# Half of retention's gate columns as four more block-product pairs, and most later modulation columns made in attention

## The chip, the cores and the metric

The kernel runs on one core of a Trainium2 chip. The metric is the device time of one execution in microseconds; 2243.01 us is the median of three runs of the kernel before (2242.38 to 2244.39). Five engines of the core run their own instruction queues and wait for each other by semaphores: TensorE (PE) multiplies, VectorE (DVE) and ScalarE (ACT) do elementwise work, GpSimd (POOL) does some elementwise work and issues some DMAs, SyncE (SP) issues nearly all other DMAs. Each engine takes its instructions in the order in which the program wrote them.

## The reference, cut to what matters

One decoder block in float32 over 1024 tokens of width 1024. The parts that the change touches:

```python
mod = jax.nn.silu(c) @ w_ada + b_ada                    # 6 x 1024 modulation columns
sh1, sc1, g1, sh2, sc2, g2 = jnp.split(mod, 6, axis=-1)
h = modulate(rms_norm(x, norm1_g), sh1, sc1)
parts = jnp.split(h @ w_in, IN_OFFSETS, axis=-1)
rq, rk, rv, rg = parts[0], parts[1], parts[2], parts[3] # rg: 4 heads x 512 gate columns
ro = retention(rotary(rq), rotary(rk) / 16, rv)         # 4 heads, chunks of 128 tokens, a running state
ro = group_norm(ro) * gn_g + gn_b
ret_out = (jax.nn.silu(rg) * ro) @ w_ret_out
att_out = dilated attention of 3 groups x 4 heads       # from parts[4:13]
merged = sigmoid(gate_a) * ret_out + sigmoid(gate_b) * att_out
x = x + g1 * (merged @ w_o)
x = x + g2 * (relu(modulate(rms_norm(x), sh2, sc2) @ w1) ** 2 @ w2)
```

Of `mod`, only sh1 and sc1 are needed at the start; the other four (32 tiles of 128 columns, `later_mods`) are first read after attention.

## The kernel before

**Precision.** Every float32 product is made of three matmuls on rounded operands: each operand is split into a high part (`hi`, rounded by a ScalarE copy) and a low part (`lo = x - hi`, a VectorE subtraction), and `mm3` (L197 to L205) adds lo*hi, hi*lo and hi*hi in PSUM. A weight tile of 128x1024 is split so by `split_w` (L188): one ScalarE copy (L191), one VectorE subtraction (L192).

**Stages in order of time.** Attention values (`av_step`); block products (`queries_keys`, running `PAIRS` through the `Blocks` class `BA`); retention values (`values`); retention itself, 4 heads of 8 chunks (`chunk`); attention, two pairs of heads (`att_step`, `cover_step`, `gate_step`); output projections; MLP.

**Block products.** A pair is 256 columns of `h @ w`. Instead of eight half-size products `Blocks` makes seven (`ORDER`, with sums of the operands), each of four groups of three matmuls 128x128x512, so 84 matmuls for a pair; the plain way (`proj_mm`) takes 96 for the same columns. `PAIRS` has 18 pairs: 8 of retention's queries and keys (`r`), 6 of attention's queries (`a`), 4 of the branch gates (`g`). `a_out` (L902) writes a pair's result; gates get a sigmoid and go to DRAM.

**Retention, one chunk** (`chunk`, L673). TensorE runs in this order: the state's products of this chunk `kv` (6 matmuls), a part of the gate projection `rg` (`proj_mm`), the scores `sT` and transposed keys `kT` of the next chunk (`s_kt`), the output `o` (9 matmuls), the transposes `oT` of the chunk before, another part of `rg`. VectorE runs in this order: the state's update (L699), the loads prepared ahead (a split of a gate weight tile, a modulation column), `sm`, `sml`, `kl` of the next chunk's scores and keys, `statel` (L713), the group norm's statistics and its result `onm` (L723 to L729), and in four chunks of each later head the product with the gate (L670). PSUM tiles of kind `s` are a ring of four, six are taken per chunk; `sT` of the next chunk takes the bank of the `o` that `onm` of the chunk before has read. Each head has four gate weight tiles (128 columns each, two chunks for a tile, 24 matmuls per chunk), and each chunk one modulation column (`mod_prep`, L450: one VectorE pass of 128x1024 and two small instructions).

**Loads.** `Steps` (L48) issues all weight, query and modulation loads in one flat order through a ring `raw` of three buffers of 128x1024 (512 KB); a load is issued when the one three places earlier has been used. Before a step's body, `prepare` uses the loads of the next step, and then the next step's successor's loads as long as these are weights. What it writes for ScalarE and VectorE (splits, `q_prep`, `mod_prep`) stands ahead of the body's own instructions.

**Attention.** `combos` gives six steps to each pair of heads. Step i makes the keys of combination i (`proj_gen`, 48 matmuls, then `k_split`: `kh` on ScalarE, `kl` on VectorE L1213) and, woven between them, the scores of combination i-1 (`scores_gen`), whose biases VectorE adds (L1243); `scores_end` takes maxima (VectorE) and exponentials (ScalarE, L1266). A step i > 0 loads a weight tile and the queries of combination i-1 (`q_prep`: `qh` L1203, `ql` L1204). After combinations 1 and 3 `stats_out` writes the statistics to DRAM and reads them back on SP's queue (L1324, L1325): the second waits there until the first has landed. During the first pair of heads `result_sums` runs sums of retention's results between DRAM tensors on POOL's DMA queue.

Of the kernel before, what the change touches and what calls it, by code (L numbers as in the profile page):

```python
# [11 lines left out]
F32 = mybir.dt.float32  # L12
# [5 lines left out]
P = 128  # L18
# [116 lines left out]
def block_kernel(ctx, tc, io, stop=None, dbg=None):  # L135
# [36 lines left out]
    dsh = cst.tile([P, NK // 2], F32, name="dsh")  # L172

# [141 lines left out]
    cb = right0.tile([P, 1024], F32, name="cb")  # L315
# [206 lines left out]
    def etile(name, dt=F32):  # L522
        return R["p"].tile([P, 1024], dt, tag="E", bufs=12, name=name)
# [149 lines left out]
    def chunk(h, c, ahead, w=None):  # L673
# [19 lines left out]
        if g > 0:  # L693
            proj_mm(hd["rgp"], hd["rgw"], ks[:2])
# [23 lines left out]
        if g > 0:  # L718
            proj_mm(hd["rgp"], hd["rgw"], ks[2:])
# [161 lines left out]
    PAIRS = [{"r": r_pairs, "a": a_pairs, "g": g_pairs}[i].pop(0) for i in "rargrargrargrargaa"]  # L881
# [3 lines left out]
    def a_load(q, part):  # L885
        pair = PAIRS[q]
        src = io[{"g": "w_gate2", "a": "w_aq"}.get(pair[0]) or f"w_r{pair[1]}"]
# [19 lines left out]
    def a_out(q, n, x, y=None):  # L907
# [12 lines left out]
        f = AF.Sigmoid if pair[0] == "g" else AF.Copy  # L920
        if y is None:
            nc.scalar.activation(o, view(x), f)
        else:
            (nc.vector.tensor_add if n == "12" else nc.vector.tensor_sub)(o, view(x), view(y))
            if pair[0] == "g":
                nc.scalar.activation(o, o, f)
        if n in ("12", "21"):
            if pair[0] == "g":
                dst = gate_d[GATES[2 * pair[1] + i]]
            elif pair[0] == "a":  # L930
                dst = aq_d[pair[2], pair[1], i]
            else:
                return
            nc.sync.dma_start(dst, OA[q][i])
# [15 lines left out]

    gate_d = [dram.tile([P, S], F32, name=f"gated{i}") for i in range(16)]
# [375 lines left out]
    def weights(pair):  # L1327
# [5 lines left out]
        pr = p.tile([P, 3, 8, 2], F32, tag="pr", name=f"pr{pair}")  # L1333
        sm = p.tile([P, 8, 2], F32, tag="ssum", name=f"ssum{pair}")
# [6 lines left out]
        for g in range(3):  # L1341
            nc.vector.tensor_mul(pr[:, g], wt[:, g], stn[g][:, :, 2:4])
        nc.vector.tensor_add(sm, pr[:, 0], pr[:, 1])
        nc.vector.tensor_add(sm, sm, pr[:, 2])
# [1058 lines left out]
def pack(x, c, w_ada, b_ada, norm1_g, w_in, rel_bias, ret_gn_g, ret_gn_b,  # L2403
# [3 lines left out]
    att = w[:, 6144:10752].reshape(1024, 3, 3, 512)  # L2407
    gates = lambda js: np.concatenate([w[:, 10752 + P * j:10752 + P * j + P] for j in js], axis=1)
# [12 lines left out]
        "w_rg": _cols(w[:, 4096:6144]),  # L2421
# [31 lines left out]
```

## Time and profile before

| what | value |
|---|---|
| median of three runs | 2243.01 us |
| the profiled execution, span | 2248.9 us |
| granted TensorE clock, mean | 0.993 |
| block products, first to last matmul | 159.5 to 503.8 us |
| retention, first `kv` to the first matmul of attention | 676.1 to 982.5 us |
| key steps of the first pair of heads, to the first gate matmul behind them | 982.5 to 1070.4 us |
| key steps of the second pair, to the first gate matmul behind them | 1142.3 to 1230.9 us |

The profile is of one execution, 2248.9 us from its first to its last instruction, 5.9 us (0.26%) over the median of the timed runs. A row of the instruction view gives start, duration, engine, line, operation, output and inputs, and in brackets how long the engine stood idle before it and who ended that. A row of the waits view gives who waited for whom: total us, times, longest. A row of the windows view gives the busy time of PE, PE's weight loads, DVE, ACT and POOL in a stretch, the granted clock and the DMA share. Durations of neighbours on one engine overlap a little, so costs are best read from start to start.

### The profile page before, as it was taken

How to read it: one execution, taken by the hardware profiler on the slowest of the kernel's cores; microseconds unless marked ns; L12 is line 12 of the kernel's file. 1: busy time of each engine (PE TensorE's matmuls, PEld its weight loads, DVE VectorE, ACT ScalarE, POOL GpSimd, SP SyncE). 2: the span in 40 equal slices, each digit the busy share in tenths (PEclk: the TensorE clock that was granted, in tenths of full speed). 3: DMA queues.
4: the chain of work that ended last, by engine and by line, in shares of the span. 5: the costliest groups of instructions: out<-in, count | busy, mean ns of one | idle time of the engine just before them, and what ended most of it. 6: DMA issues, size and time to landing. Idle time of an engine off the chain costs nothing.

```text
span 2248.9 us, 27131 instructions
## 1 busy us (share of the span) xinstructions
PE 2183.6 (97%) x10130; PEld 1808.0 (80%) x10130; DVE 1455.3 (65%) x2285; ACT 908.6 (40%) x1665; POOL 145.6 (6%) x168
## 2 busy tenths in 40 slices
PE   7999999999999999999999999999999999999998
PEld 5887888887877888887788788888778888888887
DVE  6527777753548778853554554576866665787845
ACT  4323333223334445534634633434454445533412
POOL 0001111000011122100000000002100000000003
PEclk9999999999999999999999999999999999999999
DMA  9648999625775556549723345645134443745322
GB/s 361 197 145 277 289 284 287 198 93 178 246 271 169 168 181 206 191 165 241 207 78 94 105 178 210 247 156 178 61 136 155 155 155 145 266 151 169 122 85 76
DMA packets 154371, 408.93 MB, mean 182 GB/s; under 512 B 27062, under 2 KB 54973, under 8 KB 149822
## 3 DMA queue, kind: packets, MB, share of 16 engines
q1 hardware_dynamic: 148542, 363.14, 46.3%
q0 software_dynamic: 5696, 44.04, 8.2%
q8 instruction: 80, 1.31, 0.2%
q14 instruction: 53, 0.43, 0.1%
HBM read 316.27 MB, written 156.13 MB: 210 GB/s over the span
## 4 chain that ended last, share of the span: by engine, by line
PE 47%; DVE 5%; ACT 2%; DMA 2%; issue 1%; SPq 0%; POOL 0%; POOLq 0%; DVEq 0%; ACTq 0%
PE fp L201 4%; PE fp L203 4%; PE fp L205 4%; PE f2a L203 2%; PE f2a L205 2%; PE f2a L201 2%; PE ak L201 1%; PE ak L203 1%; PE ak L205 1%; PE wo L201 1%; PE wo L205 1%; PE wo L203 1%; PE roa L203 1%; PE roa L201 1%; PE roa L205 1%
## 5 line engine op out<-in xcount | busy, mean ns | idle before, releaser
L201 PE MATMUL qap<-hh,qaw 128*128 128x512 f32 x216 | 84.3, 390 | 3.9 <-ACT qat L280 2.2
L205 PE MATMUL qap<-hh,qaw 128*128 128x512 f32 x216 | 84.1, 389 | 0.0
L203 PE MATMUL qap<-hl,qaw 128*128 128x512 f32 x216 | 84.0, 389 | 0.0
L614 POOL TENSOR_TENSOR j<-qk,j 128x512 fp32r<-128x512 f32 x32 | 43.4, 1356 | 470.2 <-ACT j L613 470.2
L1912 ACT ACTIVATE a<-a 128x512 f32<-128x512 f32 x48 | 30.3, 631 | 79.1 <-DVE a L1911 79.1
L1266 ACT ACTIVATE P<-P,ng 128x128 f32<-128x128 f32 (+1 forms) x96 | 41.9, 438 | 41.8 <-DVE ng L1263 41.8
L1809 POOL TENSOR_TENSOR accnf<-accnf,sqnf 128x256 f32<-128x256 f32 (+1 forms) x18 | 16.6, 922 | 619.0 <-ACT sqnf L1808 619.0
L258 DVE TENSOR_TENSOR fw<-w1r,fw 128x512 fp32r<-128x512 f32 x48 | 33.0, 688 | 36.3 <-ACT fw L248 36.3
L2098 ACT CAST w2h<-w2s 128x512 fp32r<-128x512 f32 x36 | 22.4, 621 | 77.6 <-DVE w2s L2136 75.3
L201 PEld LDWEIGHTS qap<-hh,qaw 128*128 128x128 f32 x216 | 40.5, 188 | 13.2 <-ACT qat L280 2.6
L201 PE MATMUL fp<-h2h,fw 128*128 128x512 f32 x128 | 50.0, 390 | 0.0
L203 PE MATMUL fp<-h2l,fw 128*128 128x512 f32 x128 | 49.8, 389 | 0.0
L205 PE MATMUL fp<-h2h,fw 128*128 128x512 f32 x128 | 49.8, 389 | 0.0
L201 PE MATMUL roa<-rh,rwl 128*128 128x512 f32 x128 | 49.8, 389 | 0.0
L203 PE MATMUL roa<-rl,rwh 128*128 128x512 f32 x128 | 49.8, 389 | 0.0
L205 PE MATMUL roa<-rh,rwh 128*128 128x512 f32 x128 | 49.8, 389 | 0.0
L636 ACT COPY sm<-sT 128x128 f32<-128x128 f32 x32 | 8.5, 267 | 101.8 <-PE sT L627 100.1
L1647 DVE TENSOR_TENSOR rwl<-rwl,rwh 128x1024 fp32r<-128x1024 f32 x25 | 30.2, 1221 | 29.0 <-ACT rwh L1677 29.0
L1809 POOL TENSOR_TENSOR accn<-accn,sqn 128x512 f32<-128x512 f32 x12 | 15.5, 1296 | 491.8 <-ACT sqn L1808 491.8
L205 PEld LDWEIGHTS qap<-hh,qaw 128*128 128x128 f32 x216 | 40.5, 188 | 8.4
L203 PEld LDWEIGHTS qap<-hl,qaw 128*128 128x128 f32 x216 | 40.5, 188 | 8.3
L1204 DVE SCALAR_TENSOR_TENSOR ql<-raw,qh 128x1024 fp32r<-128x1024 f32 x12 | 14.7, 1224 | 47.6 <-ACT qh L1203 47.6
(3081 smaller groups left out, 7216.7 us busy)
## 6 DMA issues: line engine op xcount, KB each, us to landing
v<-vd SPq DMA_DIRECT2D x32, 512.0 KB, 5.4
raw<-in_w_ada_dram SPq DMA_DIRECT2D x32, 512.0 KB, 4.9
w1r<-in_w_ff_dram SPq DMA_DIRECT2D x32, 512.0 KB, 5.1
vd<-vo SPq DMA_DIRECT2D x24, 512.0 KB, 6.4
yt<-y POOLq DMA_DIRECT2D x6, 2048.0 KB, 15.0
xsd<-as SPq DMA_DIRECT2D x24, 512.0 KB, 2.7
w2r<-in_w_ff2s_dram SPq DMA_DIRECT2D x24, 512.0 KB, 7.1
em<-in_w_ada_dram SPq DMA_DIRECT2D x16, 512.0 KB, 10.2
```

Of the source, the lines that this page charges most:

```text
L201: nc.tensor.matmul(o, wl, xh, start=first, stop=False, skip_group_check=skip)
L203: nc.tensor.matmul(o, wh, xl, start=False, stop=False, skip_group_check=skip)
L205: nc.tensor.matmul(o, wh, xh, start=False, stop=last, skip_group_check=skip)
L258: nc.vector.tensor_sub(t[:, 512:], src, fv(t[:, :512]))
L614: nc.gpsimd.tensor_sub(t[:, 1], src, fv(t[:, 0]))
L636: nc.scalar.copy(sm, ps[:, :C])
L1204: nc.vector.scalar_tensor_tensor(lo, raw, QSCALE, fv(hi), op0=ALU.mult, op1=ALU.subtract)
L1266: nc.scalar.activation(v, v, AF.Exp, bias=ng[:, blk:blk + 1], accum_out=st[:, g, blk, 2 + a:3 + a])
L1647: nc.vector.tensor_sub(lo, fv(lo), fv(hi))
L1809: (nc.vector if f == 7 else nc.gpsimd).tensor_add(G["acc", key], G["acc", key], sq)
L1912: nc.scalar.activation(o, o, AF.Relu)
L2098: nc.scalar.copy(hi, src)
```

## The change

Each head's 512 gate columns are cut in two. The first 256 stay in retention as two weight tiles instead of four; a tile now serves four chunks, with 12 matmuls per chunk instead of 24. The other 256 become one pair for each head in the block products, kind `s`, with a Silu at the end; the results go to DRAM (`srg_d`) and are read back in chunks 4 and 5 of the head. `PAIRS` has 22 entries instead of 18, in another order. Modulation columns are loaded with chunks 2, 5 and 7 of a head (12 in all) and two each with steps 1 to 5 of both attention pairs (20). The tile `cb` (Silu of c) lives on into attention, and two small tiles of `weights` are folded into others to make room.

```diff
+    cb = cst.tile([P, 1024], F32, name="cb")
...
-    cb = right0.tile([P, 1024], F32, name="cb")
...
-        if c % 2 == 0:
+        if c % 4 == 0:
             hd["rgw"] = w
             hd["rgp"] = ps_mm(f"rg{h}{c}")
-        ks = range(4 * (c % 2), 4 * (c % 2) + 4)
+        if c in (4, 5):
+            hd["srg", h, c - 2] = etile(f"srg{h}{c - 2}")
+            nc.sync.dma_start(hd["srg", h, c - 2], srg_d[h][c - 4])
+        ks = range(2 * (c % 4), 2 * (c % 4) + 2)
...
-            proj_mm(hd["rgp"], hd["rgw"], ks[:2])
+            proj_mm(hd["rgp"], hd["rgw"], ks[:1])
...
-            proj_mm(hd["rgp"], hd["rgw"], ks[2:])
+            proj_mm(hd["rgp"], hd["rgw"], ks[1:])
...
-        if c % 2 == 1:
-            hd["srg", h, c // 2] = etile(f"srg{h}{c // 2}")
-            nc.scalar.activation(hd["srg", h, c // 2], flat(hd["rgp"]), AF.Silu)
+        if c % 4 == 3:
+            hd["srg", h, c // 4] = etile(f"srg{h}{c // 4}")
+            nc.scalar.activation(hd["srg", h, c // 4], flat(hd["rgp"]), AF.Silu)
...
-    PAIRS = [{"r": r_pairs, "a": a_pairs, "g": g_pairs}[i].pop(0) for i in "rargrargrargrargaa"]
+    s_pairs = [("s", h) for h in range(H)]
+    PAIRS = [{"r": r_pairs, "a": a_pairs, "g": g_pairs, "s": s_pairs}[i].pop(0) for i in "rsrarsrarsrarsraggagga"]
...
-        f = AF.Sigmoid if pair[0] == "g" else AF.Copy
+        f = {"g": AF.Sigmoid, "s": AF.Silu}.get(pair[0], AF.Copy)
...
-            if pair[0] == "g":
+            if pair[0] in "gs":
                 nc.scalar.activation(o, o, f)
...
+            elif pair[0] == "s":
+                dst = srg_d[pair[1]][i]
...
+    srg_d = [[dram.tile([P, S], F32, name=f"srgd{h}{i}") for i in range(2)] for h in range(H)]
...
-                      ([wsplit(io["w_rg"][4 * h + c // 2])] if c % 2 == 0 else []) + [mod_load(later_mods[8 * h + c])],
-                      manual=True)
+                      ([wsplit(io["w_rg"][2 * h + c // 4])] if c % 4 == 0 else []) +
+                      ([mod_load(later_mods.pop(0))] if c in (2, 5, 7) else []), manual=True)
...
-                      ([(aq_d[pair, *combos[i - 1]], q_prep(pair, *combos[i - 1]))] if i > 0 else []),
+                      ([(aq_d[pair, *combos[i - 1]], q_prep(pair, *combos[i - 1]))] if i > 0 else []) +
+                      [mod_load(later_mods.pop(0)) for _ in range(2 if i > 0 else 0)],
                       manual=i == pair == 0)
```

More of the change, by code (lines that the diff above doesn't have):

```diff
@@ L886, in a_load @@
         pair = PAIRS[q]
-        src = io[{"g": "w_gate2", "a": "w_aq"}.get(pair[0]) or f"w_r{pair[1]}"]
+        src = io[{"g": "w_gate2", "a": "w_aq", "s": "w_rg2"}.get(pair[0]) or f"w_r{pair[1]}"]
         i = 2 * pair[1] + pair[2] if pair[0] == "a" else pair[-1]
@@ L1332, in weights @@
         wt = p.tile([P, 3, 8, 2], F32, tag="wt", name=f"wt{pair}")
-        pr = p.tile([P, 3, 8, 2], F32, tag="pr", name=f"pr{pair}")
-        sm = p.tile([P, 8, 2], F32, tag="ssum", name=f"ssum{pair}")
         wg = p.tile([P, 2, 8, 2], F32, tag="wg", name=f"wg{pair}")
@@ L1341, in weights @@
         for g in range(3):
-            nc.vector.tensor_mul(pr[:, g], wt[:, g], stn[g][:, :, 2:4])
-        nc.vector.tensor_add(sm, pr[:, 0], pr[:, 1])
-        nc.vector.tensor_add(sm, sm, pr[:, 2])
+            nc.vector.tensor_mul(stn[g][:, :, 2:4], wt[:, g], stn[g][:, :, 2:4])
+        sm = mx
+        nc.vector.tensor_add(sm, stn[0][:, :, 2:4], stn[1][:, :, 2:4])
+        nc.vector.tensor_add(sm, sm, stn[2][:, :, 2:4])
         nc.vector.reciprocal(sm, sm)
@@ L2420, in pack @@
         "w_rv": _vblocks(w[:, 2048:4096]),
-        "w_rg": _cols(w[:, 4096:6144]),
+        "w_rg": _cols(rg[:, :, :256].reshape(1024, 1024)),
+        "w_rg2": _pairs(rg[:, :, 256:].reshape(1024, 1024)),
         "w_aq": _pairs(att[:, :, 0].reshape(1024, 1536)),
```

1 line of the change is left out of this document (added).

## The prediction

> **What bounds the kernel now.** First the page's busy times, then the windows of the stages that the change touches.
>
> ```profile
> span 2248.9 us, 27131 instructions
> ...
> PE 2183.6 (97%) x10130; PEld 1808.0 (80%) x10130; DVE 1455.3 (65%) x2285; ACT 908.6 (40%) x1665; POOL 145.6 (6%) x168
> ```
>
> ```profile
> 160.00:503.00 343.00, 339.08 (x1495) 280.12 (x1494) 246.33 (x386) 103.54 (x178) 33.88 (x48) 1.00 0.78 243
> 753.00:830.00 77.00, 77.00 (x378) 64.00 (x377) 62.42 (x132) 37.27 (x93) 15.17 (x16) 1.00 0.58 192
> 985.00:1070.00 85.00, 78.17 (x402) 65.87 (x400) 36.96 (x41) 37.74 (x94) 5.78 (x7) 0.99 0.89 256
> 1070.00:1073.00 3.00, 2.59 (x6) 2.15 (x7) 2.92 (x5) 1.22 (x2) 0.00 (x0) 0.50 0.89 350
> 1073.00:1076.00 3.00, 3.00 (x9) 2.29 (x9) 3.00 (x6) 0.00 (x0) 0.00 (x0) 0.54 0.22 11
> ```
>
> TensorE is busy all through block products (first window) and all through a head of retention (second, 77.0 us for eight chunks). So fewer matmuls are a gain as long as the other engines keep up. VectorE's 62.42 of 77.0 us is the number to watch: that is far above its mean share. The third window, the first half of attention, has a TensorE that idles 7 us, and DMA engines at 0.89. The last two stand for the clock, and are used below.
>
> **Block products: four pairs more, +76.2 us.** The first of the sums' matmuls of one pair and of the fourth pair after it:
>
> ```profile
> L201 PE MATMUL qap<-xat,qaw1s x12: 389/389/389, 185.8 to 193.3; 128*128 128x512 f32 x12
> ...
> L201 PE MATMUL qap<-xat,qaw5s x12: 389/389/389, 262.0 to 269.5; 128*128 128x512 f32 x12
> ```
>
> Four pairs take 262.0 - 185.8 = 76.2 us, 19.05 each, or 0.227 us per matmul with 84 in a pair (389 ns is one's latency; the pipeline overlaps them). The new pairs have a gate pair's work, with Silu for Sigmoid, and stand between `r` pairs as `a` and `g` did, so their sums, splits and results stay hidden as those of the 18 do: VectorE has 97 of 343 us free. Bounds 75 to 80, the upper one a microsecond of uncovered split per pair.
>
> **Retention: -53 us, not the -87 that its matmuls give.** 12 matmuls fewer in each of 32 chunks are 384 x 0.227 = 87 us. Against the 4 x 84 = 336 matmuls added above, that would leave 48 x 0.227 = 11 us of gain. But VectorE has to run a chunk in the same time. Its waits in that head, and the start-to-start costs of what it loses:
>
> ```profile
> DVE gr L727 <- POOL gr L726: 5.2, 8, 0.7
> DVE sml L640 <- ACT smh L639: 2.9, 8, 0.4
> DVE sm L637 <- ACT sm L636: 2.3, 3, 1.4
> DVE state L697 <- PE kv L205: 1.0, 1, 1.0
> DVE statel L713 <- ACT stateh L712: 0.2, 1, 0.2
> DVE bn L723 <- PE o L205: 0.2, 1, 0.2
> ```
>
> ```profile
> 802.71 1.22 DVE L192 TENSOR_TENSOR raw_5999l<-raw,raw_5999h 128x1024 fp32r<-128x1024 f32 x1
> 803.84 1.22 DVE L453 SCALAR_TENSOR_TENSOR raw<-raw,cb 128x1024 f32<-128x1024 f32 x1
> ...
> 805.18 0.28 DVE L637 TENSOR_TENSOR sm<-sm,sT 128x128 f32<-128x128 f32 x1
> ```
>
> Only the waits that TensorE ends (`sm`, through ScalarE's copy of the scores, `state` and `bn`) are slack: 3.5 us in a head. Those for POOL's power and for ScalarE's roundings come in every chunk and stay. So VectorE already needs 77.0 - 3.5 = 73.5 of each 77.0 us. A split costs 1.13 us (802.71 to 803.84), a modulation column 1.34 (803.84 to 805.18). A head loses two splits and five columns, 2.3 + 6.7 = 9.0, which leaves 64.5. TensorE alone would need 77.0 - 96 x 0.227 = 55.2. So VectorE sets the pace, and TensorE feels it in the bank that `sT` takes from `o`: it can't run ahead of `onm`. Bounds for a head: 64.5 with no wait for TensorE, 68.0 with all of today's. I take 65.5, near the lower, since TensorE now has time in hand except where a head begins. Head 0 has no gate products, four passes of a split's size less: 61. Together 61 + 3 x 65.5 = 257.5, against 4 x 77.0 = 308: -50.5. And 12 gate matmuls fewer stand ahead of the first `kv`: -2.7. Sum -53, bounds -58 to -42. Reading the gates back (8 x 512 KB) comes a chunk or more ahead of its use, on SP's queue, which loses 28 loads of the same size in this stage.
>
> Blocks and retention together: +23 us.
>
> **Attention: 20 modulation columns, +43 us.** VectorE has room for 20 x 1.34 = 27 us (it is busy 36.96 of 85). The cost is where they stand. With four loads in a step and three buffers, the weight tile of the step after next is issued only when this step's queries have been used; before, it was issued a step earlier. Its split stands ahead of the step's bias adds and of `kl`, for which the next scores wait. In the changed program VectorE's order in a step is `ql`, two columns, the split, the adds, `kl`, maxima, and ScalarE's is exponentials, `qh`, the split's copy, `kh`; each turn so holds one whole DMA. From before:
>
> ```profile
> 996.13 1.22 DVE L1204 SCALAR_TENSOR_TENSOR ql<-raw,qh 128x1024 fp32r<-128x1024 f32 x1
> ...
> 1022.96 1.88 DVE L1243 TENSOR_TENSOR P<-sc,bias 128x512 f32<-128x512 f32 x3
> 1024.75 1.22 DVE L1213 TENSOR_TENSOR kl<-ak,kh 128x1024 fp32r<-128x1024 f32 x1
> ...
> 1032.54 1.23 DVE L1204 SCALAR_TENSOR_TENSOR ql<-raw,qh 128x1024 fp32r<-128x1024 f32 x1 [4.64 <-ACT qh L1203]
> ```
>
> ```profile
> L201 PE MATMUL ak<-hh,raw_8007l x16: 389/389/453, 1008.2 to 1021.3; 128*128 128x512 f32 x16
> L201 PE MATMUL ak<-hh,raw_8152l x16: 389/389/453, 1022.5 to 1035.0; 128*128 128x512 f32 x16
> ```
>
> ```profile
> raw<-in_w_ak_dram SPq DMA_DIRECT2D x1, 512.0 KB, 9.0
> raw<-in_w_ak_dram SPq DMA_DIRECT2D x3, 512.0 KB, 3.6
> ```
>
> From `kl` to the end of `ql` 9.0 us (1024.75 to 1033.77), then the load, L, then 2.2 for copy and split and 1.8 for the adds: 13.0 + L to the next `kl`. TensorE's step is 14.3 (1008.2 to 1022.5). L is 9.0 in the first pair of heads (the upper row, issued at 1021.9) and 3.6 in the second (the lower): turns of 22 and 16.6 us. To that comes SP's wait for the statistics, which now stands ahead of the weight tile of step 5:
>
> ```profile
> SPq L1325 <- DMA std<-st: 30.9, 2, 18.8
> ...
> 1051.49 1.69 SPq L85 DMA_DIRECT2D raw<-aqd  x1
> ...
> 1064.83 1.06 ACT L1203 ACTIVATE qh<-raw 128x1024 fp32r<-128x1024 f32 x1 [7.90 <-DMA raw<-aqd]
> ...
> 1070.41 1.19 PE L201 MATMUL gate<-hh,raw_8402l 128*128 128x512 f32 x2 [6.58 <-DVE raw_8402l L192]
> ...
> std<-st SPq DMA_DIRECT2D x1, 16.0 KB, 3.8
> ```
>
> Before the change this wait (18.8 us, 12.1 the second time) already holds up a load of queries and with it 6.6 us of TensorE. With L = 9, on the clock of before: queries issued at 998.6 (996.13 + 1.14 + 1.34), landed, rounded and used 11.2 later, weight load 9.0, split and adds 4.0: `kl` of step 1 at 1023, of step 2 at 1045. The exponentials end 6.7 after that (9.0 less `qh` and `ql`), the statistics land 12 to 19 later, the load takes 9.0, split and adds 3.5: `kl` of step 3 at 1076 to 1083. TensorE then still has two thirds of a step and a whole one, 24 us, so the first gate matmul starts at 1100 to 1107 instead of 1070.4: +30 to +37. With L = 3.6 and the shorter wait it is about +11. I take +30, near the upper end: 9.0 is the load row under the same sums on POOL's queue, but these may be ending by the last load. In the second pair a turn of 16.6 for 14.3 costs 2.3, the statistics' 3.8 ahead of a load as much again on top of a second such turn, 4.5, and the split at the head of step 0 stands ahead of the copies of ScalarE with its load just issued, 3.5. A stop as long as the 6.58 us one is followed by a granted clock of 0.50 and 0.54 in two windows of 3 us, which is nearly 3 us lost beyond it; once in the second pair makes it 13 (bounds 0 to 20), and in the first it is hidden, as the loads set the time. The sum for attention is +43, bounds +11 to +57.
>
> The Trainium skill (TensorE: Matmul & The Clock Gate, "Part 1: The HAM clock gate") says that TensorE falls to half rate after an idle window of about 3.4 us; the two windows agree. By that rule retention's pauses, 1.3 us a chunk, would leave the clock alone and only attention's stops are paid for twice, which speaks against loading attention with anything that waits.
>
> **Sum.** 76 - 53 + 30 + 13 = +66 on the profiled execution's 2248.9 us. I put the same +66 on the timed median, 2243 (the profiled execution was 5.9 us longer): 2309 us.
>
> **Rivals.** (1) The matmul count decides: VectorE's loop falls below TensorE's 6.9 us per chunk, and attention hides the columns: 2243 - 11 = 2232, faster. For it speaks TensorE's 97%, against it 73.5 of 77.0 us: VectorE would have to lose 18 us in a head, not 9, and it decides only below 55.2 us per head. (2) Retention as forecast, attention nearly free, because loads land in 4 us and the statistics are quick: 2243 + 23 + 0 to 15 = 2266 to 2281. For it: VectorE idles half of the time there. Against it: the order of the changed program, with the late split ahead of `kl`. (3) The first pair's loads are slower still, as those issued behind the statistics were (1051.49 to 1064.83 is 13.3): 4.3 more in each of three turns and the longer statistics' wait, 20 in all: 2330. (4) Retention's pauses halve the clock for good: 6.9 us of TensorE per chunk become 13.8, 442 us against 258, so 2493. For it only the 0.50 after a stop; no row shows the clock fall at pauses of a microsecond.
>
> **How the numbers follow.** The forecast, 2285 to 2325 with its own bounds, has a chance of 0.60; rival 2 has 0.22, rival 3 (2325 to 2350) 0.12, rival 1 0.04, rival 4 0.02. The range goes from rival 2's lower end to most of rival 3: 2264 to 2345. Under 0.2% (4.5 us) a measurement of this kernel can't tell a change. Faster is rival 1 (0.04), within 0.2% what lies between it and rival 2 (0.02), slower the rest (0.94).
>
> **What would show it.** Right: a pair of block products at 19.05 us; heads of retention at 64 to 68 us with VectorE hardly waiting for `kv` or `o`, and TensorE waiting for `onm` through `sT`; in attention TensorE's longest waits on `kl`, and ScalarE's split copies waiting for weight loads. Wrong: retention's heads at 55 to 58 us (then VectorE's loop is misread), or key steps of 14 us in the first pair of heads (then the ring of loads has more slack than I give it).

## The result, and the profile after

The changed kernel takes 2325.03 us (median of 4 runs, 2320.16 to 2327.32) against 2242.70 us (4 runs, 2241.69 to 2244.39): 82 us more, a ratio of 1.0363 (of the means) with a 95% interval of 1.0345 to 1.0381. The forecast was 2309 us, in a range from 2264 to 2345.

The page of the changed kernel (span, and busy time with share and number of instructions):

```profile
span 2325.5 us, 27170 instructions
...
PE 2198.7 (95%) x10082; PEld 1813.7 (78%) x10082; DVE 1486.2 (64%) x2341; ACT 920.8 (40%) x1697; POOL 145.2 (6%) x168
```

TensorE does 48 instructions fewer and is busy 15 us longer, in a span 77 us longer: the time is in stops and in a slower clock. The windows of four stages (time, length, busy time of PE, PE's weight loads, DVE, ACT and POOL, granted clock, DMA share, GB/s) show where: block products, the third head of retention, and the first pair of heads in two halves.

```profile
160.00:579.00 419.00, 415.12 (x1830) 343.06 (x1829) 288.25 (x450) 131.70 (x226) 33.88 (x48) 1.00 0.69 219
868.50:933.50 65.00, 59.14 (x283) 47.74 (x282) 53.70 (x114) 33.34 (x90) 14.96 (x17) 0.97 0.57 185
996.30:1054.00 57.70, 43.75 (x200) 36.20 (x199) 27.22 (x39) 20.12 (x38) 4.64 (x6) 0.88 0.81 257
1054.00:1128.00 74.00, 46.95 (x216) 39.38 (x215) 28.20 (x41) 19.66 (x58) 2.82 (x3) 0.79 0.81 228
```

Block products are as full as before. A head of retention takes 65.0 us instead of 77.0. In the key steps TensorE is busy 44 of 58 and 47 of 74 us, at a clock of 0.88 and 0.79. VectorE's waits in that head, and then TensorE's (who waited for whom: total, times, longest):

```profile
DVE gr L730 <- POOL gr L729: 5.4, 8, 0.8
DVE sml L640 <- ACT smh L639: 2.9, 8, 0.4
DVE statel L716 <- ACT stateh L715: 0.5, 2, 0.3
```

```profile
PE o L202 <- DVE state L702: 4.0, 4, 1.3
PE kT L632 <- DVE onm L732: 1.5, 3, 0.5
```

VectorE waits for POOL and ScalarE as in the kernel before and no longer for TensorE; TensorE waits for VectorE in nearly every chunk, 5.5 us in all. In the first pair of heads ScalarE's longest waits are these, and below them stand TensorE's:

```profile
ACT raw_8440h L192 <- DMA raw<-in_w_ak_dram: 23.0, 1, 23.0
ACT raw_8204h L192 <- DMA raw<-in_w_ak_dram: 13.3, 1, 13.3
ACT raw_8320h L192 <- DMA raw<-in_w_ak_dram: 12.6, 1, 12.6
```

```profile
PE sc L202 <- ACT kh L1219: 30.3, 3, 15.2
PE sc L204 <- DVE kl L1220: 10.7, 4, 3.0
```

`raw_...h` is the copy of a split, the reader of a weight tile. ScalarE stands on the tile's load 12 to 23 us, and `kh`, which stands behind it in ScalarE's order and needs nothing of that load, comes as late. TensorE's 30.3 us are put down to `kh`; the cause is one instruction ahead of it. SyncE's issues beside two of ScalarE's instructions show the lateness:

```profile
1024.74 0.33 SPq L85 DMA_DIRECT2D raw<-in_w_ak_dram  x1
...
1073.31 0.63 SPq L1331 DMA_DIRECT2D std<-st  x1
1086.39 0.38 SPq L1332 DMA_DIRECT2D stn<-std  x1
1086.87 0.52 SPq L85 DMA_DIRECT2D raw<-in_w_ak_dram  x1
```

```profile
1036.74 1.04 ACT L192 CAST raw_8204h<-raw 128x1024 fp32r<-128x1024 f32 x1 [13.28 <-DMA raw<-in_w_ak_dram]
1037.69 1.00 ACT L1219 CAST kh<-ak 128x1024 fp32r<-128x1024 f32 x1
```

The load is issued at 1024.74 and used at 1036.74, 12.0 us later, with nothing in between on ScalarE. Ahead of the weight tile of step 5 the write of the statistics (1073.31) holds SyncE's queue for 13.1 us, and the weight load behind it goes out at 1086.87.

In the second pair one stop stands out, in step 0 (TensorE, and two windows around it):

```profile
1208.59 0.48 PE L1408 MATMUL pv<-pth020(0, 0, 0)_9420,vl 128*128 128x128 f32 x1 [5.69 <-DVE vl L1303]
```

```profile
1197.60:1206.00 8.40, 5.30 (x29) 4.08 (x27) 4.25 (x8) 3.33 (x5) 0.00 (x0) 1.00 0.65 223
1206.00:1214.00 8.00, 5.41 (x19) 4.72 (x20) 4.87 (x6) 2.89 (x5) 0.00 (x0) 0.51 0.51 175
```

TensorE waits 5.69 us for the split of the values. Ahead of that split VectorE has two columns and the split of step 1, whose load has only just been issued (1200.71); e3_no_loads below tells the two apart. The clock behind the stop is 0.51.

**The kernel before, profiled again.** One of the experiments below is a second profile of the kernel before. It is 9.5 us shorter than the first:

```profile
span 2239.4 us, 27131 instructions
```

```profile
PE sc L203 <- DVE kl L1213: 0.4, 1, 0.4
```

```profile
SPq L1325 <- DMA std<-st: 13.8, 2, 10.0
```

TensorE's only wait between 982 and 1070 us is 0.4 us: the stop of 6.58 us and the half clock behind it, both among the rows of the forecast, are not there. SyncE's wait for the statistics is 10.0 us at its longest instead of 18.8, short enough to be hidden. The table gives the stages of all profiles, in us, from the first matmuls of each stage: retention from the first `kv` to the first `ak`, key steps of the first pair to the first `gate`, gates to the second pair, second pair to its first `gate`.

| kernel | retention | first pair | gates | second pair | span | median, ratio to before (95%) |
|---|---|---|---|---|---|---|
| before, first profile | 306.3 | 87.9 | 71.9 | 88.6 | 2248.9 | 2243.0 |
| before_again | 306.3 | 80.7 | 69.8 | 88.6 | 2239.4 | 2241.2 (one run) |
| changed | 253.3 | 131.5 | 69.8 | 110.0 | 2325.5 | 2325.0, 1.036 (1.035 to 1.038) |
| e1_cols_back | 276.5 | 80.7 | 69.8 | 88.6 | 2278.0 | 2280.3, 1.016 (1.014 to 1.018) |
| e2_move_only | 304.1 | 129.6 | 69.8 | 105.1 | 2301.4 | 2304.9, 1.027 (1.024 to 1.030) |
| e3_no_loads | 252.9 | 86.1 | 74.3 | 96.3 | 2270.9 | 2272.7, 1.012 (1.010 to 1.014) |
| e7_sums_late | 252.8 | 131.7 | 69.8 | 106.5 | 2323.6 | 2323.3, 1.034 (1.032 to 1.037) |
| e7b_sums_gate | 252.9 | 97.9 | 69.8 | 104.4 | 2301.3 | 2302.5, 1.027 (1.025 to 1.029) |
| e5_one_col | 267.1 | 102.8 | 70.2 | 93.1 | 2293.9 | 2296.6, 1.024 (1.023 to 1.026) |
| e12_cols_first | 253.0 | 121.8 | 69.8 | 99.7 | 2307.5 | 2312.5, 1.032 (1.030 to 1.034) |
| e13_one_col_stats | 265.4 | 91.4 | 76.7 | 91.7 | 2287.5 | 2288.4, 1.021 (1.019 to 1.022) |
| e9_stats_late | 306.3 | 80.7 | 70.4 | 88.6 | 2240.7 | 2243.8, 1.001 (1.000 to 1.002) |
| e4b_place | 306.3 | 86.7 | 71.9 | 88.6 | 2246.1 | 2248.2, 1.003 (1.002 to 1.004) |
| e10_place_stats | 307.9 | 85.6 | 69.8 | 88.6 | 2245.9 | 2247.2, 1.002 (1.001 to 1.003) |

From the second profile of before to the changed kernel the spans differ by 86.1 us: first `kv` 66.9 later (676.16 to 743.01), retention -53.0, first pair +50.8, gates 0, second pair +21.4.

### The profile page after: what moved, and what is told of

Read it like the earlier page. It is cut to its first block, busy times and chain, and to the rows that moved or that the text cites. A ratio compares the mean times of both kernels' runs of the same rounds, so it can differ in the third digit from the quotient of the medians.

```text
span 2325.5 us, 27170 instructions
## 1 busy us (share of the span) xinstructions
PE 2198.7 (95%) x10082; PEld 1813.7 (78%) x10082; DVE 1486.2 (64%) x2341; ACT 920.8 (40%) x1697; POOL 145.2 (6%) x168
## 4 chain that ended last, share of the span: by engine, by line
PE 44%; DVE 6%; DMA 4%; ACT 3%; issue 1%; POOL 0%; SPq 0%; POOLq 0%; DVEq 0%; ACTq 0%
PE fp L202 4%; PE fp L204 4%; PE fp L206 4%; DMA raw<-in_w_ak_dram 2%; PE f2a L204 2%; PE f2a L206 2%; PE f2a L202 2%; ACT P L1273 1%; PE wo L202 1%; PE wo L204 1%; PE wo L206 1%; PE roa L206 1%; PE roa L204 1%; PE roa L202 1%; PE ak L202 1%; PE ak L204 1%
## 5 line engine op out<-in xcount | busy, mean ns | idle before, releaser
L202 PE MATMUL qap<-hh,qaw 128*128 128x512 f32 x264 | 102.9, 390 | 3.9 <-ACT qat L281 2.2
L204 PE MATMUL qap<-hl,qaw 128*128 128x512 f32 x264 | 102.7, 389 | 0.0
L206 PE MATMUL qap<-hh,qaw 128*128 128x512 f32 x264 | 102.7, 389 | 0.0
L1919 ACT ACTIVATE a<-a 128x512 f32<-128x512 f32 x48 | 30.3, 632 | 78.7 <-DVE a L1918 78.7
L202 PEld LDWEIGHTS qap<-hh,qaw 128*128 128x128 f32 x264 | 49.5, 188 | 15.0 <-ACT qat L281 2.6
L202 PE MATMUL sc<-kh,ql 128*128 128x256 f32 (+1 forms) x96 | 28.3, 295 | 33.2 <-ACT kh L1219 33.2
L206 PEld LDWEIGHTS qap<-hh,qaw 128*128 128x128 f32 x264 | 49.5, 188 | 10.3
L204 PEld LDWEIGHTS qap<-hl,qaw 128*128 128x128 f32 x264 | 49.6, 188 | 10.2
L259 DVE TENSOR_TENSOR qaw<-wa,qaw 128x512 fp32r<-128x512 f32 x66 | 45.1, 687 | 14.9 <-ACT qaw L249 14.5
L2105 ACT CAST w2h<-w2s 128x512 fp32r<-128x512 f32 x36 | 22.4, 621 | 78.0 <-DVE w2s L2143 76.2
L249 ACT CAST qaw<-wa 128x512 fp32r<-128x512 f32 x66 | 39.7, 617 | 24.9 <-PE qap L206 22.3
```

The lines of the kernel that those rows point to most:

```text
L202: nc.tensor.matmul(o, wl, xh, start=first, stop=False, skip_group_check=skip)
L204: nc.tensor.matmul(o, wh, xl, start=False, stop=False, skip_group_check=skip)
L206: nc.tensor.matmul(o, wh, xh, start=False, stop=last, skip_group_check=skip)
L249: nc.scalar.copy(t[:, :512], src)
L259: nc.vector.tensor_sub(t[:, 512:], src, fv(t[:, :512]))
L1919: nc.scalar.activation(o, o, AF.Relu)
```

## The experiments

### The two halves of the change, one at a time

e1_cols_back is the changed kernel with the columns where they were:

```diff
-                      ([mod_load(later_mods.pop(0))] if c in (2, 5, 7) else []), manual=True)
+                      [mod_load(later_mods[8 * h + c])], manual=True)
...
-                      [mod_load(later_mods.pop(0)) for _ in range(2 if i > 0 else 0)],
```

> The changed kernel with all 32 modulation columns back in retention, one with each chunk as before the change, and none in attention. Theory (VectorE's work sets a head of retention; attention's extra 65 us is the columns' alone): five columns of 1.34 us come back to a head, so heads of 71 to 73 us instead of the changed kernel's 65, the first 67 instead of 60; key steps of 88 us in each pair of heads as before the change, and the 72 us between them; in all 2325 - 63 + 28 = 2290, bounds 2282 to 2296. Rival (a head is set by something else than VectorE's sum, such as the power on POOL or TensorE's order): heads stay at 65 and the total is 2262. Rival (attention's extra time came with the other parts of the change, the place of the tiles or the gates' order, not with the columns): attention stays at 311 us and the total is above 2340.

e2_move_only is the kernel before with the columns moved, and with the places of `cb` and the two small tiles that go with it:

```diff
-                      ([wsplit(io["w_rg"][4 * h + c // 2])] if c % 2 == 0 else []) + [mod_load(later_mods[8 * h + c])],
+                      ([wsplit(io["w_rg"][4 * h + c // 2])] if c % 2 == 0 else []) + ([mod_load(later_mods.pop(0))] if c in (2, 5, 7) else []),
...
+                      [mod_load(later_mods.pop(0)) for _ in range(2 if i > 0 else 0)],
```

> The kernel before with nothing but the columns moved: 12 in retention, 20 in attention as in the changed kernel, gates and pairs as before. Theory: TensorE's 77.0 us stay the limit of a head of retention (VectorE's need falls from 73.5 to 66.8 us, which buys nothing), and attention costs what it costs in the changed kernel, 65 us more less 2: 2243 + 63 = 2306, bounds 2298 to 2312. Rival (VectorE holds a head at 77.0 already before the change): heads of 70 us and a total near 2280. Rival (part of attention's extra time belongs to the changed gates): a total under 2290 with heads of 77.

Both came out nearly as the theory said. 2304.9 us lies inside its bounds; 2280.3 us is 1.7 below the lower one, since the expectation still counted 88 us for the first pair, as in the first profile of before. In e1_cols_back attention has not a microsecond of extra time (80.7, 69.8, 88.6, as in the second profile of before), so all of it belongs to the moved columns. Retention gets 23.2 us back for 20 columns, 1.16 each; so the gates alone save it 29.8 us (306.3 to 276.5), and only gates and columns together 53.0. Its third head, by windows, and VectorE's waits in it:

```profile
882.30:953.70 71.40, 61.90 (x284) 48.98 (x283) 60.09 (x129) 33.14 (x90) 15.14 (x17) 0.95 0.61 206
```

```profile
DVE gr L730 <- POOL gr L729: 5.4, 8, 0.8
DVE sml L640 <- ACT smh L639: 2.9, 8, 0.4
DVE statel L716 <- ACT stateh L715: 0.2, 1, 0.2
```

The head is 6.4 us longer than the changed kernel's, and VectorE's busy time 60.09 - 53.70 = 6.4 us longer, with the same waits: with half of the gates gone VectorE's loop is the pace, to the tenth of a microsecond. In e2_move_only the same columns leave retention and give back 2.2 us, since there TensorE's 77 us stand.

### What in the columns costs attention its time

e3_no_loads keeps VectorE's passes and leaves the 20 loads out:

```diff
+    def q_cols(pair, g, a):
+        q, cols = q_prep(pair, g, a), [mod_prep(later_mods.pop(0)) for _ in range(2)]
+        def prep(raw):
+            q(raw)
+            for col in cols:
+                col(raw)
+        return prep
...
-                      ([(aq_d[pair, *combos[i - 1]], q_prep(pair, *combos[i - 1]))] if i > 0 else []) +
-                      [mod_load(later_mods.pop(0)) for _ in range(2 if i > 0 else 0)],
+                      ([(aq_d[pair, *combos[i - 1]], q_cols(pair, *combos[i - 1]))] if i > 0 else []),
```

> The changed kernel without the loads of attention's 20 modulation columns; VectorE still makes 20 passes of the same size at the same places, on the queries' raw tile, so these columns of the modulation are not computed. Theory (the late weight loads set the key steps, since four loads in a step go through three buffers): with two loads in a step as before the change the weight tile comes a step ahead again, and key steps take 88 to 94 us per pair of heads: 2325 - 65 + 0 to 12 = 2260 to 2272. Rival (VectorE's 27 us of passes, standing ahead of the adds and kl, set the steps): half or more of the 65 us stays, 2293 or above. Rival (the loads' cost is the shared DMA engines' time only, 20 x 512 KB, not the ring): the extra time also goes, but weight loads then take as long from issue to landing as in the changed kernel, about 10 us.

Measured 2272.7 us, 0.7 above what the ring gives. In the changed kernel steps 1 to 5 of the first pair take 18.6, 27.1, 26.4, 34.2 and 13.8 us; here they take 18.7, 13.8, 14.3, 14.1 and 13.8. The weight loads of the first pair (KB each, median us from issue to landing), in the changed kernel and here:

```profile
raw<-in_w_ak_dram SPq DMA_DIRECT2D x5, 512.0 KB, 7.8
```

```profile
raw<-in_w_ak_dram SPq DMA_DIRECT2D x3, 512.0 KB, 9.2
```

A weight load takes no less time than in the changed kernel, and steps 2 to 5 lose next to nothing all the same: it is issued a step ahead. So lateness, not slowness, costs the time. The expectation's third case gave slow loads as the sign that the columns' loads cost the DMA engines' time alone. The sign is there, but it speaks against that case: if the twenty loads held the others up by their bytes, the others would be quicker without them.

But the passes are not free. In step 1 two of them stand ahead of `kl`, and TensorE waits for it 3.15 us (3.02 in the changed kernel, 0.34 in e1_cols_back); in step 0 of the second pair two stand ahead of the values' split, and the stop is 3.54 us:

```profile
1015.36 0.39 PE L204 MATMUL sc<-kl,qh 128*128 128x256 f32 x1 [3.15 <-DVE kl L1229]
...
1165.71 0.34 PE L1417 MATMUL pv<-pth020(0, 0, 0)_9396,vl 128*128 128x128 f32 x1 [3.54 <-DVE vl L1312]
...
1166.28 0.41 PE L1417 MATMUL pv<-pth020(0, 0, 0)_9396,vl 128*128 128x128 f32 x1
```

Behind the second a matmul of 128 columns takes 0.41 us instead of 0.22 to 0.28 at full clock. Against the second profile of before, step 1 is 4.3 us longer and step 0 of the second pair 7.7 (27.6 against 19.9). So in the second pair 7.7 of the 10.3 us that step 0 loses in the changed kernel (30.2) stay without the loads. How much the passes of step 1 cost the changed kernel, where the loads come later still, isn't shown. The 4.5 us at the gates (74.3 for 69.8) come from neither: there ScalarE waits 3.3 us for a load of gate weights, and the changed kernel loses nothing.

e12_cols_first keeps all loads and passes and changes their order in the ring:

```diff
-                      ([(aq_d[pair, *combos[i - 1]], q_prep(pair, *combos[i - 1]))] if i > 0 else []) +
-                      [mod_load(later_mods.pop(0)) for _ in range(2 if i > 0 else 0)],
+                      [mod_load(later_mods.pop(0)) for _ in range(2 if i > 0 else 0)] +
+                      ([(aq_d[pair, *combos[i - 1]], q_prep(pair, *combos[i - 1]))] if i > 0 else []),
```

> The changed kernel with the same loads, but in each attention step the two columns stand ahead of the queries in the ring. VectorE and ScalarE do the same work. Theory (the weight tile is issued when the load three places earlier has been used): that is now the first column, about 4 us earlier in the turn than the queries, so each turn that waits for a load gets some 4 us shorter where the load waits for nothing else: first pair 112 to 122 us instead of 131.5, second 98 to 105 instead of 110, total 2300 to 2314. Rival (VectorE's passes, or the rate of the DMA engines as such, set the turns): within 5 us of the changed kernel's 2325.

2312.5 us, first pair 121.8, second 99.7: within the theory's bounds, by order alone. The steps show a limit of it: 18.6, 26.8, 13.7, 37.5 us in the first pair. What one turn gains the next gives back in part, since the statistics' wait (12.2 us, 1063.05 to 1075.26 on SyncE's queue) keeps its place.

e5_one_col halves the columns in a step:

```diff
-                      ([mod_load(later_mods.pop(0))] if c in (2, 5, 7) else []), manual=True)
+                      ([mod_load(later_mods.pop(0))] if c in (1, 2, 3, 5, 7) or (c == 6 and h < 2) else []), manual=True)
...
-                      [mod_load(later_mods.pop(0)) for _ in range(2 if i > 0 else 0)],
+                      [mod_load(later_mods.pop(0)) for _ in range(1 if i > 0 else 0)],
```

> The changed kernel with one modulation column instead of two in an attention step, 10 in all, and 22 in retention. Theory (the ring): with three loads in a step and three buffers the weight tile is issued a step ahead again, so the steps hardly wait for it: key steps of 81 to 86 us in the first pair and 88 to 95 in the second; retention gets ten columns of 1.2 to 1.34 us back, 265 to 267 us instead of 253; in all 2325 - 48 - 18 + 13 = 2272, bounds 2264 to 2283. Rival (the passes of VectorE ahead of the adds and kl set the steps): half the columns, half the extra time, first pair 106, second 99, total 2302.

2296.6 us: in sum nearer to the rival's 2302 than to the theory's 2272. The steps tell more. In the second pair all of steps 1 to 5 take 13.7 or 13.8 us with their columns in them, so one pass does not set a step; what is left there is step 0 (24.4 against 19.9 in the second profile of before). In the first pair steps 3 and 4 are at 13.7 too, but step 2 takes 20.3 and step 5 28.0. Step 5 by SyncE's queue, and TensorE's waits:

```profile
1066.99 0.63 SPq L1331 DMA_DIRECT2D std<-st  x1
1083.34 0.38 SPq L1332 DMA_DIRECT2D stn<-std  x1
1083.82 1.20 SPq L85 DMA_DIRECT2D raw<-aqd  x1
```

```profile
PE sc L204 <- DVE kl L1220: 8.4, 3, 3.9
PE sc L202 <- DVE ql L1211: 8.2, 1, 8.2
```

The weights are in time now, and the queries behind the statistics (16.3 us on the queue) are what is late next. The theory had left that wait out of this kernel's sum. e13_one_col_stats takes it away:

```diff
         nc.sync.dma_start(natural(d, g, 4), blocks(A["st"][:, g], g))
-        nc.sync.dma_start(A["stn"][:, g], natural(d, 0, 4))
+        A["back"] = (g, d)
+
+    def stats_back():
+        g, d = A.pop("back")
+        nc.sync.dma_start(A["stn"][:, g], natural(d, 0, 4))
...
             if i > 0:
                 scores_end(pair, *last)
+                if "back" in A:
+                    stats_back()
                 if last[1] == 1:
                     stats_out(pair, last[0])
```

> e5_one_col (one column in an attention step, 22 in retention) with the read of the statistics issued one key step after their write, as in e9_stats_late. Theory (what is left of the extra time in e5_one_col's first pair, 102.8 us against 80.7, is mostly SyncE's 16.3 us on the write's landing with the queries of step 5 behind it, 14.2 us in that step): step 5 back at 14 to 16 us, first pair 87 to 91 us, second pair 93 as in e5_one_col, total 2296.6 - 13 = 2284, bounds 2280 to 2288. Rival (the queries' load is slow by itself under the sums, 10 us or more): step 5 stays above 22 us and the total above 2290.

Step 5 falls from 28.0 to 16.9 us and the first pair from 102.8 to 91.4, each a little above what was expected; 6.5 us of it come back at the gates (70.2 to 76.7), and the total is 2288.4, a hair over the bound. It is a version of the change with half of the columns and neither of attention's two long waits, and still 2% above the kernel before.

### Why the first pair is so much slower than the second

e7_sums_late calls `result_sums` at the start of the second pair's first gate step instead of in `att_step`:

```diff
                 u_final(H - 1)
-                result_sums()
...
             if n == 0:
+                if pair == 1:
+                    result_sums()
                 v_fetch(pair, 1)
```

> The changed kernel with the sums of retention's results, which run between DRAM tensors on POOL's queue during the first pair of heads, moved to the steps after the first pair's gates. Theory (the first pair is slower than the second because these sums stretch the loads to 10 to 12 us and the statistics' round trip to 13): in the first pair loads of about 4 us, turns of about 18 us instead of 26, the wait for statistics about 4 us, key steps of about 105 us instead of 131.5; at most 5 us of it is lost again where the sums now run: 2325 - 20 to 27 = 2298 to 2305. Rival (loads are slow for another reason, such as the keys' tiles and queries stored just before): the first pair stays at 125 us or above and the total within 6 us of 2325.

No change, and no evidence either: POOL has nothing else in its queue there, so the first sum went out at 1011.4 us, against 1012.1 in the changed kernel. A place in the program is a place in time only behind something on the same engine. e7b_sums_gate puts that something there, one line ahead of the call:

```diff
+                    nc.gpsimd.tensor_copy(dsh[:, 0:1], A["st"][:, 0, 0, 0:1])
                     result_sums()
```

> The changed kernel with the sums of retention's results held back for good: a small copy on POOL, which reads the second pair's maxima, stands ahead of them on POOL's queue, so they start near 1300 us instead of 1011 and run beside the second pair's gates. (In e7_sums_late they had moved in the program's order only; POOL has nothing else to do there, and their first issue stayed at 1011.4 us.) Theory (the first pair of heads is slower than the second because the sums stretch the loads): loads of 4 to 6 us, statistics back in about 4 us, first pair at 100 to 110 us instead of 131.5, the rest of attention as before or, where the sums now run, up to 10 us longer; in all 2295 to 2312. Rival (loads of 8 to 12 us have another reason): the first pair stays above 122 us and the total at 2320 or above.

2302.5 us, the first pair 97.9 instead of 131.5. The weight loads of the first pair, and the statistics on SyncE's queue:

```profile
raw<-in_w_ak_dram SPq DMA_DIRECT2D x5, 512.0 KB, 3.6
```

```profile
1053.07 0.63 SPq L1331 DMA_DIRECT2D std<-st  x1
1057.04 0.39 SPq L1332 DMA_DIRECT2D stn<-std  x1
```

3.6 us instead of 7.8, and 4.0 instead of 13.1. So the sums stretch the loads and the statistics; in the ring without slack that is 33.6 us, more than was expected. What is left of the first pair's extra time, 17.2 us (97.9 against 80.7), is close to the second pair's 15.8 (104.4 against 88.6), so the sums are the difference between the pairs. Of the gain the kernel gives back 15 us at the end, not the 10 at most that were expected (from the second pair's first gate matmul on it takes 1033.0 instead of 1017.9 us), where the sums now run; TensorE's longest wait there is 7.8 us, for the scaled exponentials.

### The start of retention, and the stop in the first profile

before_again is the kernel before, unchanged.

> The kernel before, profiled a second time. The profile from which the forecast was made is 5.9 us above the median, and its first pair of heads holds a stop of 6.58 us ahead of the first gate matmul. Theory (that stop belongs to that one execution, since e1_cols_back has no such stop with the same attention, and since taking the wait away in e9_stats_late left the median where it was): no stop, a first pair of 80.6 to 82 us instead of 87.9, a span of 2237 to 2243. Rival (it is in nearly every execution): 87 to 88 us again and a span near 2247.

As the theory said. Of 25 timed runs of the kernel before that stand beside e9_stats_late, one is longer than 2245 us (2249.7). Whether such longer runs hold this stop isn't shown, since none of them has a profile but the first. e9_stats_late is the kernel before with the edit of e13_one_col_stats:

> The kernel before, with the read of the statistics issued one key step after their write, so that SyncE's queue never stands on the write's landing (18.8 us in the first pair) with loads behind it. Theory (the only long stop of TensorE in attention, 6.58 us before the first gate matmul, comes from that wait, and the half clock after it with it): no stop there, 6 to 9 us less, 2234 to 2238, ratio 0.996 to 0.9975. Rival (the load of queries behind it is slow by itself, 13.3 us, under the sums): the stop stays at 4 us or more and the time within 3 us of the kernel before.

The first pair is at 80.7 us, but so it is without the edit, and the time is the same (ratio 1.0008, 1.0000 to 1.0017). The expectation took the profiled execution for the typical one.

e4b_place is the kernel before with another place for some tiles:

```diff
         R["sl"] = R["p"].tile([P, 2, DV], F32R, name="statel")
+        hd["on", 0] = [etile(f"on0{e}") for e in range(4)]
...
-        if c == 0:
+        if c == 0 and h > 0:
             hd["on", h] = [etile(f"on{h}{e}") for e in range(4)]
```

> The kernel before, with retention's first result tiles given their place before the scores' tiles, so that the first scores' tile no longer lies on a tile of retention's values that is still being written to DRAM. Theory (in the kernel before ScalarE's first copy of scores waits 1.7 us for that write and the first gate matmuls 4.6 us behind it; the changed kernel has no such wait, and this, not the columns, gave it some 6 us at the start of retention that the forecast did not have): the wait is gone, 3 to 6 us less, 2237 to 2240, ratio 0.997 to 0.9985. Rival (the start of retention waits for the loads of queries, keys and values in any case): no change, ratio 1.000.

The wait is gone and the time is longer by 0.3%. ScalarE's first copy of scores in the second profile of before, and in e4b_place; and a wait of e4b_place in attention:

```profile
665.83 0.27 ACT L636 COPY sm<-sT 128x128 f32<-128x128 f32 x1 [1.86 <-DMA vd<-vr]
```

```profile
662.38 0.26 ACT L637 COPY sm<-sT 128x128 f32<-128x128 f32 x1
```

```profile
ACT kh L1213 <- DMA y<-on: 3.6, 1, 3.6
```

The first `kv` comes 2.8 us earlier (673.3 against 676.2). But the tiles that moved now lie where attention makes its first `kh`, which waits 3.6 us until retention's last results are written out, and step 1 takes 19.0 us instead of 14.4. e10_place_stats has both edits:

> The kernel before with both edits, the place of the first result tiles and the later read of the statistics. If each acts where it is said to and neither moves the other's wait elsewhere, the gains add: 9 to 15 us less, 2228 to 2234, ratio 0.993 to 0.996. If one is only hidden behind the other's cover, about one of them stays: ratio 0.996 to 0.998.

No gain to add: 2247.2 us, e4b_place's loss and e9_stats_late's nothing. None of these kernels beats the one before.

At the start of retention the changed kernel is better than e4b_place, and the rows name a second cause. TensorE's first matmul of `rg` in the second profile of before, and in the changed kernel:

```profile
668.02 1.22 PE L201 MATMUL rg<-hh,raw_4661l 128*128 128x512 f32 x2 [4.79 <-DVE kl L647]
669.04 1.05 PE L203 MATMUL rg<-hl,raw_4661h 128*128 128x512 f32 x2
```

```profile
740.16 0.73 PE L202 MATMUL rg<-hh,raw_5201l 128*128 128x512 f32 x2 [1.71 <-DVE sm L637]
740.73 0.62 PE L204 MATMUL rg<-hl,raw_5201h 128*128 128x512 f32 x2
```

Before, it waits for `kl`, the last reader of `kT`; after, for `sm`, the reader of `sT`, which comes earlier. The stop is 1.71 instead of 4.79 us and no half clock follows (0.62 for two matmuls against 1.05). Why `rg` waits for another reader was not tried by itself; e4b_place still waits 3.3 us for `kl`, with the half clock behind it.

## Why the prediction was right or wrong, point by point

**Block products, +76.2: right.** The last matmul of the block products comes 76.2 us later (506.56 to 582.73; the 503.8 in the table ahead of the prediction is twelve matmuls earlier), and the stage is as full as before.

**Retention, -50.5 in the heads: right in mechanism, and 2.5 us too cautious.** From first `kv` to first `kv` the heads take 59.1, 65.0, 65.1 and 64.1 us (61 and three times 65.5 were given), in all 253.3 against 306.3; the forecast had 257.5 against 308. That VectorE's loop sets them is shown by e1_cols_back, that the columns alone buy next to nothing (2.2 us) by e2_move_only. Where TensorE feels that loop was foretold less well: the prediction named `onm`, through the bank of `sT`, but in the third head 4.0 us of TensorE's waits stand on `state` and 1.5 us on `onm`.

**The start of retention, -2.7: a term missing.** First `kv` came 66.9 us later instead of 73.5. The 12 matmuls were right; the shorter stop ahead of them (4.79 to 1.71) and the half clock that no longer follows were not foreseen. About 1.7 us more come from retention's values: a stop of 2.07 us stands there in either kernel, and in the second profile of before the 8 us behind it are at a clock of 0.79, in the changed kernel at 1.00. No row ties that to the change, so this part may be chance. The other two could be read as a cost in the profile of before, but not that the change would end them.

**Attention's first pair, +30: the mis-sized term.** It measured +43.6 on the profile that the forecast used, and +50.8 on a usual execution. The base is 7.2 of it: the 87.9 us held the stop that the second profile does not have. The forecast noted that its profile stood 5.9 us above the median, and put the difference on the median all the same, without asking which rows the excess was in. The other 13.6 are in the chain of loads. VectorE's `kl` of steps 1, 2 and 3 in the changed kernel:

```profile
1040.75 1.22 DVE L1220 TENSOR_TENSOR kl<-ak,kh 128x1024 fp32r<-128x1024 f32 x1
...
1066.49 1.22 DVE L1220 TENSOR_TENSOR kl<-ak,kh 128x1024 fp32r<-128x1024 f32 x1
1100.69 1.22 DVE L1220 TENSOR_TENSOR kl<-ak,kh 128x1024 fp32r<-128x1024 f32 x1
```

On the clock of before, where attention starts 13.8 us earlier (982.5 against 996.3), they are at 1027, 1053 and 1087 and the first gate matmul at 1114; the forecast had 1023, 1045, 1076 and 1100. Each stretch is 3 to 4 us too short: the first by the load (12.0 us for 9.0), the second (25.7 us for 22) by 2.4 us in its load (11.4 from the issue at 1051.1 to the split) and by 1.4 us ahead of it (10.4 us from `kl` to the issue: the forecast took 9.0 from a later step, and this one holds a table load of ScalarE of 1.28 us, as it does in the kernel before), the third by load and wait together (34.2 for 31; the 13.1 us of the statistics lay inside the 12 to 19 forecast), and the last, 27.1 for 24, stands behind a stop of 15.2 us whose half clock the forecast took for hidden.

**The cause named for it: right.** "The cost is where they stand" (a ring of three with four loads) is what e3_no_loads and e12_cols_first show and the second pair of e5_one_col bears out, and that the sums stretch L is what e7b_sums_gate shows. The trace named `kh` as the longest wait where the forecast had named `kl`: both stand behind the split, one on each engine.

**Attention's second pair, +13: mis-sized, +21.4 measured.** Step 0 was given 3.5, for a late load, and one loss of clock of 3; it measured 10.3 (30.2 against 19.9), and by e3_no_loads 7.7 of it stay without the loads. What was left out is the two columns' passes of 2.7 us ahead of the values' split, which the forecast took to fit into VectorE's idle time. Steps 3 and 4 were given 2.3 and 4.5 and measured 11.1 (15.7 and 22.8 against 13.7 each).

**The sum.** +66 was forecast. Attention was 29 us dearer on a usual execution (50.8 + 21.4 against 43), and the start and the heads of retention 9 us cheaper: +86 between those two spans, +82 between the medians. Two errors of opposite sign so brought the sum nearer than its terms. 2325.0 us stands on the line between the forecast's own bounds (2285 to 2325) and rival 3 (2325 to 2350); that the time came out no higher than this line is partly luck.

**The rivals.** (1), the matmul count, fell: 65 us per head, not 55. (2), free attention, fell. (3), slower loads, named 2330 by loads of 13.3 us; the loads (12.0, 11.4 and 10.4 us from issue to use) came out between it and the forecast, and so did the time, nearer to the rival (5 us) than to the forecast (16 us). Its longer wait for the statistics did not come (13.1 us, at the short end of 12 to 19). (4), retention's pauses halving the clock, fell: 0.97 in a head.

**What the change would give with attention for nothing.** Blocks +76.2, the start -9.3 and the heads -53.0 leave +13.9 us. A pair costs 19.05 us, and the 96 matmuls that it spares a head give back only what VectorE can follow, some 13 us in a head (53.0 / 4), even with 20 of the 32 columns gone. Fewer columns in retention were not tried.

## What to carry to other kernels

Taking work from the engine that is 97% busy pays only down to the next engine's need in that same loop; here VectorE's need stood 5% below TensorE's, and 87 us of matmuls bought 30, or 53 with 20 columns taken off VectorE as well. A load put into a ring of buffers costs by what it does to the lead of the others: count the loads between two uses against the number of buffers, since at the number plus one a latency that was hidden lies open in every turn, and whatever stretches it counts in full. Work put on an engine that is half idle can still cost what it delays: two passes of 1.34 us ahead of the one split that TensorE waited for cost 7.7. And when a profiled execution is longer than the median, find the rows that hold the excess before taking a stage of it as the base.

## What the runs showed of the hardware that was not expected

Stops of TensorE well under 6.58 us can also halve the clock. In e7b_sums_gate a stop of 2.95 us, with steady matmuls ahead of it, is followed by a window at 0.50 (clock is the column behind the five busy times):

```profile
1047.50:1050.50 3.00, 2.98 (x13) 2.89 (x14) 1.86 (x3) 1.08 (x5) 0.00 (x0) 0.50 0.00 1
```

A stop of 2.07 us stands between the first two matmuls of retention's values (`va`), behind steady block products, in the kernel before and in the changed kernel. The 3 us behind it, in the first profile of before and in the changed kernel:

```profile
509.24:512.24 3.00, 3.00 (x7) 2.44 (x8) 1.09 (x1) 0.00 (x0) 0.00 (x0) 0.50 1.01 314
```

```profile
585.41:588.41 3.00, 3.00 (x13) 2.50 (x14) 1.08 (x1) 0.00 (x0) 0.00 (x0) 1.00 1.00 324
```

Half clock in one and full clock in the other: the length of a stop alone does not decide, and a forecast can't count on either. The stop of 1.71 us at the start of the changed kernel's retention is followed by full clock too. The Trainium skill (TensorE: Matmul & The Clock Gate, "Part 1: The HAM clock gate") gives an idle window of about 3.4 us for the fall; these rows show it below that. In retention, with pauses of about a microsecond, the clock fell a little, to 0.97 and in e1_cols_back to 0.95, with no stop over 1.3 us in those heads; the rows do not say why.
